# Order of an expert's half and quarter products, and row gathers shared by two experts, in a two-layer mixture-of-experts backbone

## The chip, the cores and the metric

The kernel runs on one core of a Trainium2 chip. The metric is the device time of one execution in microseconds. The engines are called as in the profile: PE is TensorE's matmul, PEld its weight load, DVE is VectorE, ACT is ScalarE, POOL is GpSimd, SP is SyncE, which issues most of the loads. SPq and POOLq are the queues of SP and POOL.

## What is computed

Two trunk layers over 512 latent tokens and 256 context tokens of width 1024. A layer mixes its tokens (a short convolution, a chunk gating, a neighbourhood attention, a latent attention), and then sends each token to two of 32 experts. The first layer routes 768 tokens, the second 512. What matters here is the expert stage:

```
gates = p_grp * jax.nn.softmax(top_v, axis=-1)
expert_id = (g_sel * EXPERTS_PER_GROUP + top_i).reshape(-1)
...
def expert_block(args):
    xb, e = args
    return (jax.nn.silu(xb @ w_gate[e]) * (xb @ w_up[e])) @ w_down[e]
...
y = y_buf[dest].reshape(n_tok, TOP_K_INNER, d).astype(jnp.float32) * gates[..., None]
return jnp.sum(y, axis=1).astype(h.dtype)
```

`w_gate` and `w_up` are 1024 x 512 for an expert, `w_down` 512 x 1024, all float32: 6 MB an expert, 201 MB a layer.

## The kernel before

`build` runs trunk and expert stage of the first layer, then of the second. The expert stage is `moe`. The routing ranks the experts by how many tokens they have; a table `CAP` of the program gives each rank a number of rows (first layer 2152 in all, second 1640), and tokens beyond it go through a loop for overflow blocks, whose number the device finds at run time (`nov`; all engines wait for it). `R["tok"]` is a table of 128 x 32 numbers: column r holds the token of each row of rank r, and a number out of bounds where there is none.

`seq` is the order of the products: gate and up of expert e, then down of expert e - 1. `load` walks along the same order ahead of PE and issues the weights from SP (line 147 in `unit2`) into slots, as far as slots are free: tiles `u` of 512 KB, and `xa`, `xb`, `xc`, of 1 MB, that hold two units. A unit holds two k of gate or up, or one k of down; a slot is free when the last product that reads it is done. SP issues in order, so a load whose slot is not free holds up all later ones. Loads of all queues share 16 DMA engines.

For each expert, `gather` lets POOL fetch its rows from `h2d` into one of three buffers `xb` (line 1704, by the indices in `R["tok"]`). `rows` turns them (PE transposes at line 1381 into `xTw`, a DVE copy at 1383 into `XT`). `gate_up` does both products, ACT the SiLU and DVE the product of the two (lines 1430 and 1431), `hT` turns the result, `down` does the third product, `rows_out` takes it out of PSUM, and POOL scatters the rows to `yd`. The rows of the last four ranks, 32 each, don't go through `yd`, but through a table of their own (`tail_scale`, `tail_rows`), and before them a scaling row `modd` is loaded behind the last scatter.

An expert's rows are the stationary operand of its products, the weights are streamed. `parts` cuts the rows by their number:

```
n = -(-W // QW)
return {1: [(0, QW)], 2: [(0, W)], 3: [(0, HW), (HW, QW)], 4: [(0, HW), (HW, HW)]}[n]
```

with HW = 64 and QW = 32. A part of more than 32 rows takes half of the array's columns, and its output columns are cut in two that run side by side ("halves", 512 columns each); a part of 32 rows or fewer takes a quarter, and its output is cut in four ("quarters", 256 columns). `streams` gives these pieces their places. Experts of 65 to 96 rows have one part of each kind: nine of the first layer, ten of the second. In `products` the loop over k is the outer one, so such an expert does, for each k, its halves and then its quarters:

```
for k in range(K):
    for a, w, o, b, m, c in S:
```

K is 8 for gate and up, 4 for down. The order in which each engine's instructions come is settled by a scheduler when the program is built; it may move an expert's products past each other. A product of float32 shows as two records of PE.

Of the kernel before, what the change touches and what calls it, by code (L numbers as in the profile page):

```python
# [11 lines left out]
I32 = mybir.dt.int32  # L12
# [9 lines left out]
NE = 32  # L22
# [41 lines left out]
HW = 64  # L64
# [30 lines left out]
class K:  # L95
# [886 lines left out]
    def project(self, l, ap, ah, yT, yM, TQ, w, wo, yc):  # L982
# [21 lines left out]
        br = ap.tile([128, M, 36], F32, name=f"brr{l}")  # L1004
        rows = ap.tile([32, 128], F32, name=f"mrow2{l}")
        nc.gpsimd.dma_start(rows, self.modd[l][1:3].rearrange("s m (k p) -> (s m k) p", p=128))
        lg = self.lg = self.small([128, TQ, 36], f"lg{l}", bufs=1)
        a2 = [self.bc(a2[m], l, 2, m) for m in range(M)]
# [58 lines left out]
        for t in range(TQ):  # L1067
# [8 lines left out]
            if t == 1:  # L1076
                ps = self.pss("br")
                with tc.issue_after(self.lastm.ins):
                    nc.tensor.transpose(ps[:, 0:32], rows, self.ident[0:32, 0:32])
                mc = ap.tile([128, 2, 2, 8], F32, name=f"mcol2{l}")  # L1080
                nc.vector.tensor_copy(mc.rearrange("p s m k -> p (s m k)"), ps[:, 0:32])
# [290 lines left out]
    def xt_tile(self, mp):  # L1372
        return mp.tile([128, D], F32, tag="XT", name=self.nm("XT"), bufs=2)

    def rows(self, mp, X, W):

        nc = self.nc
        ps = self.psw("xTw")
        Xv = X[0:W, :].rearrange("p (d k) -> p d k", k=8)
        for k in range(8):  # L1380
            nc.tensor.transpose(ps[:, k * 128:k * 128 + W], Xv[:, :, k], self.ident[0:W, 0:W])  # L1381
        xt = self.xt_tile(mp)[:, 0:8 * W].rearrange("p (k t) -> p k t", k=8)
        nc.vector.tensor_copy(xt, ps.rearrange("p (k n) -> p k n", k=8)[:, :, 0:W])  # L1383
        return xt
# [19 lines left out]
    def products(self, x, parts, ws, n, K, name):  # L1404


        S, out = [], []
        for a, w in parts:
            ps = self.pss(name)
            st = self.streams(ps, n, w, ws)  # L1410
            S += [(a, w) + y for y in st]
            out.append((ps, [y[0] for y in st]))
        for k in range(K):
            for a, w, o, b, m, c in S:
                q = m[0].shape[1]
                self.lastm = self.nc.tensor.matmul(o, x[:, k, a:a + w], m[k // q][:, k % q, c], start=(k == 0),  # L1416
                                                   stop=(k == K - 1), tile_position=(0, b))
        return out

    def gate_up(self, mp, xt, parts, wg, wu):  # L1420
# [81 lines left out]
    def overflow(self, l, R, src, pp, mp, XB):  # L1502
# [16 lines left out]
        with tc.For_i(0, n) as i:  # L1519
# [41 lines left out]
            nc.scalar.copy(xv, pv)  # L1561
            pg, pu = self.pss("over"), self.pss("over")
            products("g", [pg], xv)
            nc.scalar.activation(hh, pg[0:W, :], AF.Silu)
            products("u", [pu], xv)
            nc.vector.tensor_mul(hh, hh, pu[0:W, :])
            pt = self.pss("over")
# [28 lines left out]
    def moe(self, l):  # L1596
        nc, A, tc = self.nc, self.A, self.tc
        T = 6 if l == 0 else 4
        NB = 2 * T
        NA = 128 * NB  # L1600
# [3 lines left out]
        pp = ctx.enter_context(tc.tile_pool(name=f"mpp{l}", reuse_waits="tile", bufs=1, side=ms))  # L1604
# [12 lines left out]
        XB = [pp.tile([128, D], F32, name=f"xb{l}_{i}") for i in range(3)]  # L1617
# [4 lines left out]
        order = [0, 1]  # L1622
# [5 lines left out]
        while any(todo):  # L1628
            i = next(i for i in (range(len(COST))[::-1] if ahead > 0 else range(len(COST))) if todo[i])
# [3 lines left out]
        cap = [CAP[l][r] for r in order]  # L1633
        parts = [self.parts(w) for w in cap]
# [11 lines left out]
        for at, ts in ((("gu", NE - 2), range(0, T // 2)), (("d", NE - 3), range(T // 2, T))):  # L1646
            i = lseq.index(at) + 1
# [33 lines left out]
        def done_with(i):  # L1681
            for x in held.pop(seq[i]):
                x[1] = False

        xt, h, ht, X, written = {}, {}, {}, {}, []
        load(2)
        with tc.tile_pool(name=f"rt{l}", reuse_waits="tile", bufs=1, side=ms) as ap, tc.high_priority():
            R, rest = self.route(l, ap, pp)
# [8 lines left out]
        mp = ectx.enter_context(tc.tile_pool(name=f"moe{l}", reuse_waits="tile", bufs=1, side=ms))  # L1697
        self.rx = self.small([128, 6], "rx", bufs=1)

        def gather(e):  # L1700

            if e < NE:
                X[e] = XB[e % 3]
                self.lastp = nc.gpsimd.indirect_dma_start(  # L1704
                    out=X[e][0:cap[e], :], out_offset=None, in_=self.h2d[l][:, :],
                    in_offset=bass.IndirectOffsetOnAxis(ap=R["tok"][0:cap[e], order[e]:order[e] + 1], axis=0),
                    bounds_check=NA // 2 - 1, oob_is_err=False)

        def rows(e):
            if e < NE:  # L1710
                xt[e] = self.rows(mp, X.pop(e), parts[e][-1][0] + parts[e][-1][1])
                gather(e + 3)

        gather(0)
        self.overflow(l, R, src, pp, mp, XB[1:])
        gather(1)
        gather(2)
        fg = None
        if l == 1:

            g2 = [self.bc(self.bc_tile(pp), l, 3, 0)]
            fg = self.bc_tile(pp)
            nc.gpsimd.dma_start(fg, A["final_norm_g"].to_broadcast([128, D]))
        rows(0)
        load()
        tt = self.tail_table(l, pp, mp, R, T)
        acc = iter(range(T))
        na = dict(zip((("gu", NE - 2), ("d", NE - 3), ("gu", NE - 1), ("d", NE - 2)), (1, T // 3, T // 3, 1)))
        for i, (m, e) in enumerate(seq):
# [6 lines left out]
            else:  # L1736
# [5 lines left out]
                if j < 0:  # L1742
                    y = self.rows_out(mp, py, parts[e], g2[0] if l else None, cap[e])
                    nc.gpsimd.indirect_dma_start(  # L1744
                        out=self.yd[l][:, :], in_=y, in_offset=None,
                        out_offset=bass.IndirectOffsetOnAxis(ap=R["dst"][0:cap[e], order[e]:order[e] + 1], axis=0),
                        bounds_check=NA - 1, oob_is_err=False)
# [21 lines left out]
        for t in range(T):  # L1769
            ps = self.psw("tailw")  # L1770
# [168 lines left out]
```

## Time and profile before

| | us |
|---|---|
| runs: median (lowest to highest, 3 runs) | 1941.24 (1935.98 to 1943.87) |
| the profiled execution | 1937.65 |
| its span | 1935.9 |
| PE busy (12876 instructions) | 1778.4 |
| DVE, ACT, POOL busy | 740.0, 466.8, 234.3 |
| mean rate of the DMA engines over the span | 290 GB/s |

The first layer's expert stage lies from about 486 to 1065 us of the span, the second's from about 1400 to 1920. All rows below are of the profiled execution. A busy share is an average over stages that have different limits; what bounds a stage is read from the stage.

### The profile page before, as it was taken

What the parts mean: (1) busy time and instruction counts of PE and PEld (TensorE: products, weight loads), DVE (VectorE), ACT (ScalarE), POOL (GpSimd) and SP (SyncE); (2) the same over time, 40 slices, a digit from 0 to 9 for tenths busy, and PEclk for the clock granted to TensorE, in tenths of its full rate; (3) what the DMA queues carried; (4) which work ended last, traced back from release to release, by engine and by line L of the source; (5) the groups of instructions that cost most, each with busy time, mean ns of one, the idle gap of its engine ahead of it and who ended that gap; (6) DMA issues with size and microseconds to landing.
All of it is one profiled execution on the core that took longest, in us unless ns stands there. A gap on an engine that the chain in (4) does not pass through costs nothing. (4 is left out here: it accounts for less than half of the span.)

```text
span 1935.9 us, 32616 instructions
## 1 busy us (share of the span) xinstructions
PE 1778.4 (92%) x12876; PEld 973.3 (50%) x12876; DVE 740.0 (38%) x1599; ACT 466.8 (24%) x842; POOL 234.3 (12%) x267
## 2 busy tenths in 40 slices
PE   6999999996999999999986999999699999988994
PEld 3788788875334433333222688776434333333331
DVE  3666466555111110211105666665523232222225
ACT  4443464222111111111102555642200000000001
POOL 1000100132111111101001001002311011111010
PEclk9999999997999999999976999999799999999997
DMA  8368965534999999999849432528399999999995
GB/s 309 94 197 287 325 217 170 207 142 184 355 384 392 397 387 375 392 388 402 324 170 371 142 88 72 156 77 306 113 362 387 400 400 398 397 382 405 403 414 242
DMA packets 167101, 561.89 MB, mean 290 GB/s; under 512 B 20642, under 2 KB 47330, under 8 KB 137888
## 3 DMA queue, kind: packets, MB, share of 16 engines
q1 hardware_dynamic: 141616, 499.68, 68.7%
q0 software_dynamic: 21152, 54.16, 8.0%
q10 hardware_dynamic: 4176, 5.91, 0.9%
q8 instruction: 104, 1.70, 0.4%
q14 instruction: 53, 0.43, 0.1%
HBM read 533.54 MB, written 35.52 MB: 294 GB/s over the span
## 5 line engine op out<-in xcount | busy, mean ns | idle before, releaser
L1416 PE MATMUL gate_up<-u,XT 128*32 128x256 f32 (+4 forms) x1664 | 287.6, 493 | 5.9 <-DMA u<-in_w_up 4.1
L1416 PE MATMUL gate_up<-xb,XT 128*32 128x256 f32 (+4 forms) x1152 | 224.4, 489 | 10.4 <-DMA xb<-in_w_up 9.1
L1430 ACT ACTIVATE eh<-gate_up 64x256 f32<-64x256 f32 (+4 forms) x87 | 43.6, 501 | 788.0 <-PE gate_up L1416 774.4
L1383 DVE COPY XT<-xTw 128x256 f32<-128x256 f32 (+6 forms) x64 | 43.9, 689 | 449.2 <-PE gate_up L1416 433.0
L1416 PE MATMUL gate_up<-xa,XT 128*32 128x256 f32 (+4 forms) x680 | 156.9, 490 | 8.6 <-DMA xa<-in_w_up 8.4
L1416 PEld LDWEIGHTS gate_up<-u,XT 128*32 128x32 f32 (+4 forms) x1664 | 82.6, 121 | 160.7 <-issue 134.6
L194 PE MATMUL zunits<-hT,hi 128*128 128x512 f32 (+1 forms) x384 | 139.8, 365 | 0.9 <-ACT cqs L688 0.8
L195 PE MATMUL zunits<-hT,hi 128*128 128x512 f32 (+1 forms) x384 | 136.0, 354 | 0.0
L196 PE MATMUL zunits<-hT,lo 128*128 128x512 f32 (+1 forms) x384 | 135.3, 352 | 0.0
L1416 PE MATMUL gate_up<-xc,XT 128*32 128x256 f32 (+4 forms) x440 | 127.3, 498 | 2.8 <-DMA xc<-in_w_up 2.1
L1704 POOL DMA_INDIRECT xb<-h2d,tok x64 | 62.1, 971 | 528.1 <-PE xTw L1381 486.8
L1416 PEld LDWEIGHTS gate_up<-xb,XT 128*32 128x32 f32 (+4 forms) x1152 | 61.9, 121 | 123.6 <-issue 100.9
L1416 PE MATMUL down<-u,ehT 128*32 128x256 f32 (+4 forms) x656 | 111.6, 514 | 7.0 <-DMA u<-in_w_down 6.1
L1744 POOL DMA_INDIRECT yd<-ey,dst x56 | 52.9, 945 | 401.8 <-ACT ey L1473 215.6
L1431 DVE TENSOR_TENSOR eh<-eh,gate_up 64x256 f32<-64x256 f32 (+4 forms) x87 | 50.5, 580 | 131.3 <-ACT eh L1430 128.1
L1416 PE MATMUL down<-xb,ehT 128*32 128x256 f32 (+4 forms) x592 | 96.4, 498 | 2.6 <-DMA xb<-in_w_down 2.4
L1475 DVE TENSOR_TENSOR ey<-down,bc 32x256 f32<-32x256 f32 (+7 forms) x112 | 57.8, 516 | 102.1 <-PE down L1416 100.9
L1381 PE MATMUL xTw<-cpack,xb 96*128 96x96 f32 (+6 forms) x512 | 72.9, 282 | 20.4 <-DVE XT L1383 8.7
L1381 PEld LDWEIGHTS xTw<-cpack,xb 96*128 96x128 f32 (+6 forms) x512 | 63.1, 201 | 55.0 <-issue 24.0
L1473 ACT COPY ey<-down 64x512 f32<-64x512 f32 (+6 forms) x102 | 50.5, 495 | 157.2 <-PE down L1416 156.1
L175 DVE TENSOR_TENSOR lo<-u,hi 128x1024 fp32r<-128x1024 f32 (+2 forms) x54 | 65.6, 1217 | 46.6 <-ACT hi L169 44.1
L1416 PEld LDWEIGHTS gate_up<-xa,XT 128*32 128x32 f32 (+4 forms) x680 | 40.2, 119 | 85.8 <-issue 70.9
(395 smaller groups left out, 2876.5 us busy)
## 6 DMA issues: line engine op xcount, KB each, us to landing
u<-in_w_gate SPq DMA_DIRECT2D x112, 512.0 KB
u<-in_w_up SPq DMA_DIRECT2D x106, 512.0 KB
u<-in_w_ada SPq DMA_DIRECT2D x96, 512.0 KB
u<-in_w_down SPq DMA_DIRECT2D x89, 512.0 KB
xb<-in_w_gate SPq DMA_DIRECT2D x37, 1024.0 KB
xb<-in_w_down SPq DMA_DIRECT2D x37, 1024.0 KB
xb<-in_w_up SPq DMA_DIRECT2D x35, 1024.0 KB
xa<-in_w_down SPq DMA_DIRECT2D x26, 1024.0 KB
```

The costliest lines, as they stand in the source:

```text
L175: self.nc.vector.tensor_sub(o, v, h.bitcast(F32))
L194: mm(out, a[0], b[0], start=start, stop=False)
L195: mm(out, a[0], b[1], start=False, stop=False)
L196: self.lastm = mm(out, a[1], b[0], start=False, stop=stop)
L1381: nc.tensor.transpose(ps[:, k * 128:k * 128 + W], Xv[:, :, k], self.ident[0:W, 0:W])
L1383: nc.vector.tensor_copy(xt, ps.rearrange("p (k n) -> p k n", k=8)[:, :, 0:W])
L1416: self.lastm = self.nc.tensor.matmul(o, x[:, k, a:a + w], m[k // q][:, k % q, c], start=(k == 0), stop=(k == K - 1), tile_position=(0, b))
L1431: self.lastv = nc.vector.tensor_mul(v, v, ps[64:64 + r, 0:c])
L1473: self.nc.scalar.copy(y[a:a + w, c], p[0:w, :])
L1475: self.nc.vector.tensor_mul(y[a:a + w, c], p[0:w, :], g2[b:b + w, c])
L1704: self.lastp = nc.gpsimd.indirect_dma_start(out=X[e][0:cap[e], :], out_offset=None, in_=self.h2d[l][:, :], in_offset=bass.IndirectOffsetOn ...
L1744: nc.gpsimd.indirect_dma_start(out=self.yd[l][:, :], in_=y, in_offset=None, out_offset=bass.IndirectOffsetOnAxis(ap=R["dst"][0:cap[e], ord ...
```

## The change

Two parts. `products` now takes the parts of an expert one after the other, with the loop over k inside: all halves of the 64 rows, then all quarters of the other 32. And rows are gathered by groups: two experts that follow each other and have at most 64 rows each form a group, any other expert is one by itself. A gather always names 128 rows. For a group of two the indices of both, 64 each, are copied by DVE into a column of a table `gi`, and the second expert's rows land on partitions 64 to 127, from where `rows` turns them. There are 26 groups in the first layer and 24 in the second, for 32 and 32 gathers before.

```diff
-    def rows(self, mp, X, W):
+    def rows(self, mp, X, a, W):
...
-        Xv = X[0:W, :].rearrange("p (d k) -> p d k", k=8)
+        Xv = X[a:a + W, :].rearrange("p (d k) -> p d k", k=8)
         for k in range(8):
-            nc.tensor.transpose(ps[:, k * 128:k * 128 + W], Xv[:, :, k], self.ident[0:W, 0:W])
+            nc.tensor.transpose(ps[:, k * 128:k * 128 + W], Xv[:, :, k], self.ident[a:a + W, a:a + W])
...
-        S, out = [], []
+        out = []
         for a, w in parts:
             ps = self.pss(name)
             st = self.streams(ps, n, w, ws)
-            S += [(a, w) + y for y in st]
+            for k in range(K):
+                for o, b, m, c in st:
+                    q = m[0].shape[1]
+                    self.lastm = self.nc.tensor.matmul(o, x[:, k, a:a + w], m[k // q][:, k % q, c], start=(k == 0),
+                                                       stop=(k == K - 1), tile_position=(0, b))
             out.append((ps, [y[0] for y in st]))
-        for k in range(K):
-            for a, w, o, b, m, c in S:
-                q = m[0].shape[1]
-                self.lastm = self.nc.tensor.matmul(o, x[:, k, a:a + w], m[k // q][:, k % q, c], start=(k == 0),
-                                                   stop=(k == K - 1), tile_position=(0, b))
         return out
...
+        groups, place, e = [], {}, 0
+        while e < NE:
+            n = 2 if e + 1 < NE and max(cap[e], cap[e + 1]) <= HW else 1
+            for i in range(n):
+                place[e + i] = len(groups), HW * i
+            groups.append(range(e, e + n))
+            e += n
...
-        def gather(e):
-
-            if e < NE:
-                X[e] = XB[e % 3]
-                self.lastp = nc.gpsimd.indirect_dma_start(
-                    out=X[e][0:cap[e], :], out_offset=None, in_=self.h2d[l][:, :],
-                    in_offset=bass.IndirectOffsetOnAxis(ap=R["tok"][0:cap[e], order[e]:order[e] + 1], axis=0),
-                    bounds_check=NA // 2 - 1, oob_is_err=False)
+        gi = pp.tile([128, len(groups)], I32, name=f"gi{l}")
+
+        def gather(g):
+
+            if g >= len(groups):
+                return
+            X[g] = XB[g % 3]
+            if len(groups[g]) == 1:
+                r = order[groups[g][0]]
+                ix = R["tok"][:, r:r + 1]
+            else:
+                ix = gi[:, g:g + 1]
+                for i, e in enumerate(groups[g]):
+                    nc.vector.tensor_copy(ix[HW * i:HW * i + HW], R["tok"][0:HW, order[e]:order[e] + 1])
+            nc.gpsimd.indirect_dma_start(out=X[g], out_offset=None, in_=self.h2d[l][:, :],
+                                         in_offset=bass.IndirectOffsetOnAxis(ap=ix, axis=0),
+                                         bounds_check=NA // 2 - 1, oob_is_err=False)
...
-                xt[e] = self.rows(mp, X.pop(e), parts[e][-1][0] + parts[e][-1][1])
-                gather(e + 3)
+                g, a = place[e]
+                xt[e] = self.rows(mp, X[g], a, parts[e][-1][0] + parts[e][-1][1])
+                if e == groups[g][-1]:
+                    gather(g + 3)
```

How the instructions move, at three places. On PE, the gate and up product of the first layer's second expert (96 rows), in the kernel before; the weights are in tiles `xa` and `xb`, 64x512 is a half and 32x256 a quarter, and x2 stands for two alike:

```order
L1416 MATMUL gate_up_5621<-xa_1_5078,XT_5598 64x512
L1416 MATMUL gate_up_5621<-xa_2_5079,XT_5598 64x512
L1416 MATMUL gate_up_5622<-xa_1_5078,XT_5598 32x256 x2
L1416 MATMUL gate_up_5622<-xa_2_5079,XT_5598 32x256 x2
L1416 MATMUL gate_up_5621<-xb_0_5082,XT_5598 64x512
L1416 MATMUL gate_up_5621<-xb_1_5083,XT_5598 64x512
L1416 MATMUL gate_up_5622<-xb_0_5082,XT_5598 32x256 x2
L1416 MATMUL gate_up_5622<-xb_1_5083,XT_5598 32x256 x2
```

and in the changed kernel:

```order
L1414 MATMUL gate_up_5624<-xa_1_5078,XT_5599 64x512
L1414 MATMUL gate_up_5624<-xa_2_5079,XT_5599 64x512
L1414 MATMUL gate_up_5624<-xb_0_5082,XT_5599 64x512
L1414 MATMUL gate_up_5624<-xb_1_5083,XT_5599 64x512
...
L1414 MATMUL gate_up_5641<-xa_1_5078,XT_5599 32x256 x2
L1414 MATMUL gate_up_5641<-xa_2_5079,XT_5599 32x256 x2
...
L1414 MATMUL gate_up_5641<-xb_0_5082,XT_5599 32x256 x2
L1414 MATMUL gate_up_5641<-xb_1_5083,XT_5599 32x256 x2
```

Before, halves and quarters take turns for each k; now sixteen halves come first, and the quarters follow.

On POOL, the first layer's gathers after the overflow loop (the DMA into `xb` from `h2d`), before:

```order
L1704 DMA xb_1_5102<-h2d_110,tok_5238 96x1024
L1704 DMA xb_2_5103<-h2d_110,tok_5238 32x1024
L1704 DMA xb_0_5101<-h2d_110,tok_5238 128x1024
L1704 DMA xb_1_5102<-h2d_110,tok_5238 64x1024
L1704 DMA xb_2_5103<-h2d_110,tok_5238 64x1024
```

and now, where `gi` in place of `tok` marks a gather for two experts:

```order
L1721 DMA xb_1_5102<-h2d_110,tok_5238 128x1024
L1721 DMA xb_2_5103<-h2d_110,tok_5238 128x1024
L1721 DMA xb_0_5101<-h2d_110,tok_5238 128x1024
L1721 DMA xb_1_5102<-h2d_110,gi_5274 128x1024
L1721 DMA xb_2_5103<-h2d_110,tok_5238 128x1024
```

The gathers name 128 rows each; the one for the two experts of 64 rows has taken the place of two.

On DVE, the end of the first layer's routing, where `nb` and `nov` lead to the number of overflow blocks, in the changed kernel; the copies into `gi` are new, and `tlim` stood ahead of `nb` before:

```order
L1330 CAST tpos_7336<-posi_5254 128x12
L1270 TENSOR_SCALAR more_5256<-cpack,col_5249 32x6
L1720 COPY gi_5274<-tok_5238 64x1 x2
L1271 TENSOR_REDUCE nb_5257<-more_5256 32x1
L1720 COPY gi_5274<-tok_5238 64x1 x4
L1275 CAST nov_5262<-route_5260 1x1
L1720 COPY gi_5274<-tok_5238 64x1 x2
L1321 TENSOR_TENSOR tlim_7121<-col_5249,cpack 32x1
L1720 COPY gi_5274<-tok_5238 64x1 x4
```

Two copies have come ahead of `nb`, four between it and `nov`, and six behind.

## Rows read from the trace of the kernel before

**Rows 1.** The page: PE's busy time; the rate in 40 equal slices.

```profile
PE 1778.4 (92%) x12876; PEld 973.3 (50%) x12876; DVE 740.0 (38%) x1599; ACT 466.8 (24%) x842; POOL 234.3 (12%) x267
...
GB/s 309 94 197 287 325 217 170 207 142 184 355 384 392 397 387 375 392 388 402 324 170 371 142 88 72 156 77 306 113 362 387 400 400 398 397 382 405 403 414 242
```

**Rows 2.** Stretches: us, busy us by engine, granted clock, DMA share, GB/s.

```profile
486.00:940.00 454.00, 446.86 (x2520) 160.41 (x2520) 66.67 (x130) 64.41 (x127) 52.47 (x55) 0.99 1.01 386
940.00:1065.00 125.00, 99.83 (x783) 32.13 (x782) 35.97 (x58) 20.55 (x35) 9.28 (x15) 0.79 0.73 275
1402.00:1705.00 303.00, 289.23 (x2350) 106.11 (x2352) 84.35 (x190) 12.51 (x27) 39.70 (x42) 0.98 1.01 390
1705.00:1912.00 207.00, 178.88 (x1148) 62.60 (x1143) 52.12 (x97) 11.19 (x22) 18.47 (x22) 0.93 1.00 401
```

**Rows 3.** Waits of PE, 500 to 990 us: total, times, longest.

```profile
PE hT L1450 <- DVE ehT L1452: 3.1, 6, 0.5
...
PE down L1416 <- DVE ehT L1452: 0.2, 1, 0.2
```

**Rows 4.** Waits of PE, 990 to 1065 us.

```profile
PE tail_scalew L1366 <- DMA u<-modd: 5.9, 1, 5.9
```

**Rows 5.** Waits of PE, 1402 to 1700 and 1700 to 1912 us: first line of each.

```profile
PE hT L1450 <- DVE ehT L1452: 6.8, 5, 1.8
...
PE gate_up L1416 <- DMA xa<-in_w_up: 8.4, 2, 7.1
```

**Rows 6.** The chain that ended last, from 1700 us: start, us, what.

```profile
1705.74 18.26 DMA xb<-in_w_down
...
1883.50 21.39 DMA xa<-in_w_up
```

**Rows 7.** Timeline of PE in a mixed expert, first layer: start, us, instruction.

```profile
840.88 0.41 PE L1416 MATMUL gate_up<-xa,XT 128*32 128x256 f32 x2
...
841.12 0.39 PE L1416 MATMUL gate_up<-xa,XT 128*32 128x256 f32 x2
...
841.45 0.64 PE L1416 MATMUL gate_up<-xa,XT 128*64 128x512 f32 x1
...
841.93 0.59 PE L1416 MATMUL gate_up<-xa,XT 128*64 128x512 f32 x1
...
842.46 0.41 PE L1416 MATMUL gate_up<-xa,XT 128*32 128x256 f32 x2
```

**Rows 8.** Timeline: halves alone; the chain: mixed product, product of quarters alone.

```profile
573.53 0.59 PE L1416 MATMUL gate_up<-xb,XT 128*64 128x512 f32 x1
...
573.96 0.59 PE L1416 MATMUL gate_up<-xb,XT 128*64 128x512 f32 x1
...
1419.07 12.70 PE gate_up L1416 x96
...
1440.97 3.45 PE gate_up L1416 x64
```

**Rows 9.** Timeline of SP's issues at the end of the first layer.

```profile
985.43 1.91 SPq L147 DMA_DIRECT2D u<-in_w_up  x2
1014.30 0.33 SPq L147 DMA_DIRECT2D xa<-in_w_down  x1
```

**Rows 10.** The page's group of gathers: busy, mean ns, idle before.

```profile
L1704 POOL DMA_INDIRECT xb<-h2d,tok x64 | 62.1, 971 | 528.1 <-PE xTw L1381 486.8
```

**Rows 11.** DMA, 479 to 484 us: packets, MB, share, of the first gather.

```profile
q0 software_dynamic: 112, 0.14, 11.8%
```

**Rows 12.** Timeline of DVE at the end of the first routing.

```profile
478.06 0.14 DVE L1321 TENSOR_TENSOR tlim<-col,cpack 32x1 f32<-32x1 f32 x1
478.18 0.15 DVE L1271 TENSOR_REDUCE nb<-more 32x1 f32<-32x6 f32 x1
478.69 0.15 DVE L1275 CAST nov<-route 1x1 int32<-1x1 f32 x1 [0.37 <-PE route L1273]
```

**Rows 13.** Waits of SP, 1440 to 1705 us: total, times, longest.

```profile
SPq L147 <- PE down L1416: 13.5, 8, 6.8
```

## The prediction

> **What bounds the kernel now.** I read four views in this order: the page's lines of busy time and of rate by slice, the busy times by stretch, the waits of TensorE (PE) in each stretch, and the chain that ended last. The page shows PE busy for 92% of the span, and rates near 400 GB/s in the slices of the two expert stages [rows 1]. An average over stages cannot say which of the two sets the time, so the stretches come next [rows 2]. In the first layer's expert stage, from 486 to 940 us, both are full: PE busy 446.86 of 454 us, DMA share 1.01. From 940 to 1065 the DMA share is 0.73, so there the loads follow PE. In the second layer's, 1402 to 1912 us, the share is 1.01 and then 1.00 to the end.
>
> The waits separate them. Between 500 and 990 us PE's waits fill six lines, 6.9 us in all, and no DMA is among them; the first and the last of the six stand in [rows 3]. So the first layer is bound by PE: whatever its products lose or gain there moves everything behind. At 996.7 PE waits for a broadcast that GpSimd (POOL) issues behind the last scatter [rows 4]; that DMA is itself late by what PE is late, and shifts with it. In the second layer PE waits for no DMA from 1402 to 1700, but after that it does, up to 7.1 us at once [rows 5], and the chain of work that ended last leaves PE at 1705.74 for a load of 18.26 us, and near the end runs over a load from 1883.50 on, 21.39 us [rows 6]. PE there runs into a DMA queue that has been full since 1402. So the second layer ends when its loads have landed.
>
> **What a change of tile shape costs.** An expert of 65 to 96 rows has a part of 64 rows (two products side by side, "halves", 512 columns) and one of 32 rows (four, "quarters", 256 columns). The kernel now does for each k the halves and then the quarters. [Rows 7] show one k-step: quarters at 840.88 and 841.12, halves at 841.45 and 841.93, quarters again at 842.46, each product in two passes. One whole step is 842.46 - 840.88 = 1.58 us. Where halves follow halves, a pass takes 573.96 - 573.53 = 0.43 us; sixteen passes of quarters alone take 3.45 us, 0.216 each [rows 8]. Without a change of shape the step would be 2 x 0.43 + 2 x 0.216 = 1.29 us. The two changes in it cost 0.29 us.
>
> **The change part by part.** *Order of products.* In the order of instructions, as it is put out for both kernels, the first layer has 121 steps from halves to quarters and 100 back before, and 47 and 26 now: 74 pairs fewer. In the second it is 132 and 114 before, 50 and 32 now: 82 fewer. (Nine and ten such experts, twelve k-steps each; the scheduler still splits a product in two where it expects its weights late, and mixes it with other products, so that not all go.) First layer: 74 x 0.29 = 21.5 us off PE, all of it where PE waits for no load: **-21.5 us**. The bounds are 0, if the loss does not go with the order, and 9 experts x 10 pairs x 0.29 = 26 us, if only one change per product were left. A few halves stand alone in both orders, without a partner on the other half of the array; I count them as equal. Second layer: 82 x 0.29 = 23.8 us off PE, beside DMA that is full: **0**. The cover is the queue of loads; where it to run faster, part of this would count (a rival below).
>
> *What is late next in the first layer.* The closest PE comes to its loads is before 940, where DMA is saturated. Two of the nine experts stand at the start (5.8 us of the 21.5), the other seven from the eighteenth expert on. After that the loads had been waiting for PE: share 0.73 in the last stretch, that is 0.27 x 125 = 34 us of idle DMA, and SyncE (SP) stands from 987.34 to 1014.30 with a load whose place PE has not freed [rows 9]. I take it that the gain passes through.
>
> *Weights are held longer.* With all halves first, the unit of weights for the first k is read until the quarters come by. In the first layer SP is then nearer to its places being free than now, since PE is earlier; 0 in the sum, priced as a rival.
>
> *Gathers.* There are 14 fewer (50 for 64). POOL takes 0.97 us for one and waits 486.8 us for PE before them [rows 10], so nothing is on the path: 0. Each now names 128 rows. A row past an expert's tokens has an index out of bounds and moves nothing of size: the first gather, of 96 rows, left 112 packets with 0.14 MB [rows 11], about 33 rows of 4 KB. So the 2608 further rows (26 x 128 - 2152 and 24 x 128 - 1640) bring next to no bytes. Bounds: nothing, or as full rows 1432 x 4 KB at 390 GB/s = 15 us in the layer where DMA is the end; I take 0, as the packets show. If the cover went, a gather that is late would hold the transposes of two experts; it is issued three groups ahead, which is more experts than now.
>
> *Transposes from the upper half.* The second expert of a pair is turned from partitions 64 on. Their number stays. No row shows this transpose there; I take 0, with bounds of a tenth of a microsecond to either side for each of the 14 pairs.
>
> *Copies of indices.* VectorE (DVE) gets 28 copies of 64 numbers. Two stand ahead of the sum of blocks and four ahead of the number of overflow blocks, on which all engines wait before the expert stage. Instructions of that size follow each other by 0.12 us, and the second place has 0.37 us of idle time in which four nearly fit [rows 12]. So 0.3 us a layer: **+0.6 us** (bounds 0 and 1.4).
>
> **Sum.** The profiled execution took 1937.65 us: 1937.65 - 21.5 + 0.6 = 1916.8. That execution lies 3.6 us under the median of the runs, and the four times shown spread over 7.9 us; I add half of the 3.6 and forecast **1919 us**.
>
> **Rivals.** *A: the second layer gains too.* For: from 1402 to 1705 DMA moves 390 GB/s, and the best slice of the page, in the same layer, 414 [rows 1, 2]. If what holds the rate down is PE's pace, the same bytes at 414 take 303 x (1 - 390/414) = 17.5 us less: 1901 us. Against: the share of 1.01 says that every engine has a packet at every moment, and SP waits there mostly for earlier loads; its largest line on PE is 13.5 us in 8 waits for the down product [rows 13]. Chance 0.12. The Trainium skill ("HBM Reference", Specifications) puts a core that streams alone at about 425 GB/s; by that figure a layer at 390 would have room for all that PE gives back, and the time would be about 1895, an estimate; no slice of this profile reaches that rate.
>
> *B: a load becomes the wait in the first layer.* PE overtakes its loads before 940, where DMA has nothing to spare. Then only the idle DMA of the last stretch counts, 34 us less the 27 of SP's long wait, which stays: a gain of 7 us, 1933 us. For: both resources are full in that stretch. Against: no wait for a load in 490 us, so there is a stock of unknown size. Chance 0.16.
>
> *C, slower: weights held to the end of a product starve the loads of the second layer.* A unit of gate or up weights (two k) is free after 2 x 1.58 = 3.2 us now, and after 8 x 0.86 + 0.15 + 2 x 0.43 = 7.9 with the change, 4.7 later; one of the down product (one k) after 4.0 in place of 1.6, 2.4 later. Ten experts: 71 us of later issue, in the layer that ends with its loads. It decides if more than 21 of these 71 us become idle DMA, that is, a share under 0.96 there; at half, 35 us: 1954 us. Against: SP has several loads under way and rarely waits for PE there [rows 13]. Chance 0.05.
>
> **How the numbers follow.** Forecast 0.67, A 0.12, B 0.16, C 0.05. A measurement of this kernel can tell about 0.5% from no change, 9.7 us, so the forecast and A are faster (0.79), B is no change (0.16), C is slower (0.05). The range reaches from A to B, 1900 to 1934, and leaves out C, the far end of A and a weaker B; the forecast's own range is 1911 to 1927, from its bounds and the spread of the runs.
>
> **What would show it.** In the profile after: a mixed expert's gate and up product takes about 10.5 us and not 12.70 [rows 8]; the expert stage of the first layer, 486 to 1065 us before, is some 21 us shorter, and PE still waits for no load in it until the broadcast; the second layer's stage, 1402 to 1912 us before, stays near 510 us with a share of 1.0, and PE's waits for loads there, few before 1700 now, grow by about 20 us and begin earlier. I am wrong if PE waits for loads in the first layer (B), if the second layer's rate rises above 400 GB/s (A), if its DMA share falls (C), or if the step from halves to quarters costs as much once per product as now in twelve.

## The result, and the profile after

The changed kernel takes **1895.09 us** (median of 4 runs, 1892.86 to 1898.18), the one before 1942.18 (4 runs): ratio **0.9764**, 95% interval 0.9738 to 0.9790. I forecast 1919 and a range of 1900 to 1934. The direction was right; the gain is twice the forecast and lies 5 us outside the range. The profiled execution took 1894.95 us, its span is 1893.2.

From the start of the first product of an expert stage to the start of the last, the first layer goes from 577.1 us (486.9 to 1064.0) to 543.2 (489.0 to 1032.2), the second from 514.1 (1402.5 to 1916.6) to 503.3 (1369.9 to 1873.2). That is -33.9 and -10.8; all that lies around the stages adds 2 us. I had -21.5 and 0.

The page after, lines of PE's busy time and of the rate by slice, answers to [rows 1]:

```profile
PE 1730.5 (91%) x12876; PEld 999.2 (53%) x12876; DVE 744.1 (39%) x1627; ACT 467.2 (25%) x842; POOL 221.7 (12%) x253
...
GB/s 305 107 188 275 318 227 184 160 211 141 339 414 407 399 398 396 398 401 411 387 229 319 147 87 106 140 76 303 129 366 411 414 410 411 404 401 404 409 414 226
```

Busy times of the stretches of both stages in the changed kernel, columns as in [rows 2]:

```profile
489.00:910.00 421.00, 418.20 (x2466) 163.64 (x2470) 63.06 (x124) 62.34 (x123) 45.89 (x48) 0.99 1.01 404
910.00:1033.00 123.00, 97.34 (x844) 38.09 (x835) 38.38 (x63) 22.73 (x40) 9.71 (x15) 0.83 0.86 323
1370.00:1660.00 290.00, 272.12 (x2352) 117.83 (x2352) 83.98 (x189) 12.53 (x27) 34.75 (x36) 0.98 1.00 403
1660.00:1873.00 213.00, 178.02 (x1172) 66.34 (x1174) 54.97 (x102) 11.21 (x22) 15.62 (x19) 0.90 0.98 395
```

PE is busy 48 us less. The line that I did not foresee is the last column: the first stretch moves 404 GB/s where it moved 386, at the same share of 1.01. The bytes are the same, 561.89 MB before and 561.90 after.

PE's timeline of the second expert of the first layer (65 to 96 rows), after: halves of gate and up, then their quarters.

```profile
503.90 3.65 PE L1414 MATMUL gate_up<-xa,XT 128*64 128x512 f32 x16
507.38 3.60 PE L1414 MATMUL gate_up<-xb,XT 128*64 128x512 f32 x16
510.92 1.93 PE L1414 MATMUL gate_up<-xa,XT 128*32 128x256 f32 x32
512.67 1.91 PE L1414 MATMUL gate_up<-xb,XT 128*32 128x256 f32 x32
```

The product lasts from 503.90 to 514.58, 10.68 us, where one of its size took 12.70 in the kernel before [rows 8]: 2.02 us, seven pairs of changes of shape at 0.29. I had said about 10.5.

PE's waits from 500 to 960 us, after, all of them; they answer to [rows 3]:

```profile
PE hT L1449 <- DVE ehT L1451: 2.6, 5, 0.5
PE xTw L1381 <- DVE XT L1383: 0.7, 1, 0.7
```

So the first layer still waits for no load, although PE is faster. In the second layer the chain leaves PE for the loads much earlier than in [rows 6], where that was at 1705.74. The chain after, rows from its stretch from 1369 us on:

```profile
1405.01 3.45 PE gate_up L1414 x64
...
1418.74 6.65 DMA xc<-in_w_up
...
1439.10 17.14 DMA u<-in_w_gate
1456.36 18.33 DMA xc<-in_w_gate
```

From 1418.74 on this chain is mostly loads. PE's waits for loads in this stage grow from 18.7 to 30.5 us in all, by 12 us and not by the 20 that I had. The second layer is bound by its loads, as I said, but its loads run faster.

**Where the rate comes from.** The view of DMA over one gather shows it. First the kernel before, 737.5 to 740.5 us, in which a gather of 80 rows lands beside the loads (packets, MB, share of the 16 engines' time):

```profile
DMA packets 236, 0.87 MB, mean 290 GB/s; under 512 B 56, under 2 KB 56, under 8 KB 204
...
q1 hardware_dynamic: 126, 0.57, 66.6%
q0 software_dynamic: 110, 0.30, 36.0%
```

Then the change, 727.3 to 730.3 us, where a gather of 128 rows for an expert of a similar size lands (some packets of a scatter are in both windows):

```profile
DMA packets 346, 1.21 MB, mean 403 GB/s; under 512 B 106, under 2 KB 106, under 8 KB 291
...
q1 hardware_dynamic: 177, 0.86, 70.3%
q0 software_dynamic: 168, 0.34, 29.5%
```

Three microseconds of 16 engines are 48. Before, the gather had 36.0% of them for 0.30 MB, or 73 rows of 4 KB: 0.24 us a row; the loads had 66.6% for 139 times 4 KB: 0.23 us each. After, it is 0.17 and 0.16 us. The engines have a packet at every moment in both, but before each packet takes 1.4 times as long, **the loads' packets as well**. Over the three microseconds the rate is 290 and not 403.

To count this over the stages I gave the packets of the gathers' queue, in order of time, to the gathers and scatters by their numbers of rows (a scatter of 40 rows that stands alone leaves 80 packets, one of 72 leaves 112, and so a number of rows that is no multiple of 16 is filled up), and took the mean time of a gather's 4 KB packets. Before it is 208 ns in both layers (172 for the first layer's gathers that name 128 rows there), after 166 and 167; the loads' packets that start while a gather's rows land took 207 and 202 ns per 4 KB before, and 162 after. The assignment is rough where a gather and a scatter overlap. The scatters name 32 to 128 rows in the first layer of both kernels and their packets take 161 to 163 ns; loads beside a scatter alone take 159 to 163 ns. In the change a scatter of 80 rows lands from 898.2 to 906 us while the DMA engines move 418 GB/s:

```profile
q0 software_dynamic: 96, 0.28, 9.1%
```

So it is the gathers, which write into the on-chip tiles, and not every transfer of fewer than 128 rows. A plainer count needs no such assignment: in the kernel before, the 4-us slices from 490 to 940 us move 377 GB/s where they hold packets of the gathers' queue and 402 where they don't; in the change, from 490 to 910, 404 and 401.

### The profile page after: what moved, and what is told of

Read it like the earlier page. It is cut to its first block, busy times and chain, and to the rows that moved or that the text cites. A ratio compares the mean times of both kernels' runs of the same rounds, so it can differ in the third digit from the quotient of the medians.

```text
span 1893.2 us, 32583 instructions
## 1 busy us (share of the span) xinstructions
PE 1730.5 (91%) x12876; PEld 999.2 (53%) x12876; DVE 744.1 (39%) x1627; ACT 467.2 (25%) x842; POOL 221.7 (12%) x253
## 2 busy tenths in 40 slices
DMA packets 169022, 561.90 MB, mean 297 GB/s; under 512 B 22562, under 2 KB 49250, under 8 KB 139808
## 4 chain that ended last, share of the span: by engine, by line
PE 25%; DMA 18%; DVE 3%; issue 3%; ACT 1%; POOL 0%; SPq 0%; POOLq 0%; ACTq 0%; DVEq 0%
DMA u<-in_w_down 6%; PE gate_up L1414 6%; PE down L1414 3%; DMA u<-in_w_gate 3%; PE zunits L194 2%; PE zunits L195 2%; PE zunits L196 2%; DMA u<-in_w_up 2%; DMA xb<-in_w_down 2%; DMA xb<-in_w_up 1%; DMA xa<-in_w_up 1%; PE transP L838 1%; DMA xc<-in_w_gate 1%; DMA xc<-in_w_up 1%; PE tailw L1791 1%
## 5 line engine op out<-in xcount | busy, mean ns | idle before, releaser
L1414 PE MATMUL gate_up<-u,XT 128*32 128x256 f32 (+4 forms) x1664 | 277.3, 489 | 12.3 <-DMA u<-in_w_up 9.2
L1414 PE MATMUL gate_up<-xb,XT 128*32 128x256 f32 (+4 forms) x1152 | 215.0, 483 | 12.0 <-DMA xb<-in_w_up 10.6
L1414 PEld LDWEIGHTS gate_up<-u,XT 128*32 128x32 f32 (+4 forms) x1664 | 92.2, 123 | 149.3 <-issue 106.9
L1414 PE MATMUL gate_up<-xa,XT 128*32 128x256 f32 (+4 forms) x680 | 149.8, 488 | 5.3 <-DMA xa<-in_w_up 2.9
L1414 PEld LDWEIGHTS gate_up<-xb,XT 128*32 128x32 f32 (+4 forms) x1152 | 69.1, 121 | 112.1 <-issue 80.1
L1414 PE MATMUL down<-xb,ehT 128*32 128x256 f32 (+4 forms) x592 | 91.9, 490 | 5.6 <-DMA xb<-in_w_down 5.6
L1381 PEld LDWEIGHTS xTw<-cpack,xb 96*128 96x128 f32 (+6 forms) x512 | 61.7, 200 | 51.8 <-issue 22.8
L1381 PE MATMUL xTw<-cpack,xb 96*128 96x96 f32 (+6 forms) x512 | 72.1, 283 | 17.7 <-DVE XT L1383 7.0
L175 DVE TENSOR_TENSOR lo<-u,hi 128x1024 fp32r<-128x1024 f32 (+2 forms) x54 | 65.5, 1217 | 46.0 <-ACT hi L169 45.4
L194 PEld LDWEIGHTS zunits<-hT,hi 128*128 128x128 f32 x384 | 72.8, 190 | 16.0 <-issue 4.4
L1451 DVE COPY ehT<-hT 128x256 f32<-128x256 f32 (+4 forms) x47 | 19.6, 418 | 154.2 <-PE hT L1449 153.7
```

Source lines behind the costliest of these rows:

```text
L175: self.nc.vector.tensor_sub(o, v, h.bitcast(F32))
L194: mm(out, a[0], b[0], start=start, stop=False)
```

## The experiments

**Theory.** Two gains. The order of products takes some 24 us of PE off the first layer. Gathers of fewer than 128 rows slow the packets in flight, and 128 rows end that. **Rivals:** the rate rises since PE comes earlier (my rival A); or what counts is that there are 14 gathers fewer.

The first four runs part these. All stage times below go from the start of the first expert product to the start of the last.

**1. The order alone.**

```diff
 kernel before, products():
-        for k in range(K):
-            for a, w, o, b, m, c in S:
+            for k in range(K):
+                for o, b, m, c in st:
```

> The new order of products with the gathers of before. Theory (two separate gains: the order takes some 24 us of PE off the first layer's stage; gathers of fewer than 128 rows slow all packets in flight, and 128 rows end that): the rate stays as before, near 386 and 390 GB/s in the two expert stages, a 4 KB packet of a gather takes about 190 ns; first layer's products 15 to 30 us shorter, second layer's stage still 510 to 516 us; 1912 to 1925 us. Rival A (the rate follows PE's pace): rate 402 in both stages, second stage near 503 us, 1893 to 1900 us.

Measured: 1921.18 us, ratio 0.9905 (0.9887 to 0.9922); stages 559.0 and 512.6 us. Rival A falls: 380 us of the second stage (the busy times from 1444 us on, columns as in [rows 2]) run at 399 GB/s,

```profile
1444.00:1824.00 380.00, 342.75 (x2383) 132.60 (x2383) 93.96 (x202) 15.66 (x33) 41.94 (x44) 0.98 1.01 399
```

and the same stretch of the kernel before at 398:

```profile
1460.00:1840.00 380.00, 356.25 (x2460) 126.20 (x2458) 96.95 (x210) 16.03 (x34) 43.98 (x46) 0.98 1.01 398
```

The gathers' packets still take 206 and 205 ns. And PE now meets its loads in the first layer; its waits for DMA from 500 to 975 us:

```profile
PE gate_up L1414 <- DMA xc<-in_w_up: 2.4, 1, 2.4
PE down L1414 <- DMA xb<-in_w_down: 1.4, 3, 0.5
PE gate_up L1414 <- DMA xb<-in_w_gate: 1.3, 2, 0.7
PE gate_up L1414 <- DMA xb<-in_w_up: 0.9, 2, 0.6
```

That is 6.0 us, where neither the kernel before nor the change has any. The stage is 18.1 us shorter, with these waits in it: this is the mechanism of my rival B, a load that becomes the wait, in a small size.

**2. The gathers alone.**

```diff
 changed kernel, products(): as in the kernel before
-            for k in range(K):
-                for o, b, m, c in st:
+        for k in range(K):
+            for a, w, o, b, m, c in S:
```

> The new gathers with the order of products of before. Theory: rate of the second layer's stage 400 to 405 GB/s and the stage 8 to 14 us shorter than before; first layer's stage within 6 us of before, since PE sets it; packets of a gather about 162 ns; 1925 to 1934 us. Rival A: rate 386 to 391 as before, 1938 to 1944 us.

Measured: 1930.40 us, ratio 0.9946 (0.9927 to 0.9964); stages 574.8 and 508.2 us; the gathers' packets 165 and 171 ns. Busy times of 380 us in the second stage:

```profile
1460.00:1840.00 380.00, 359.93 (x2518) 127.59 (x2506) 99.32 (x215) 16.41 (x35) 38.33 (x40) 0.98 1.01 408
```

So the gathers alone lift the rate from 398 to 408. The second stage gains 5.9 us, less than I wrote down. The first, where PE sets the time, gains 2.3.

Alone the parts give 19.3 and 10.0 us, together 45. The rest is that they need each other, in the first layer above all: 18.1 and 2.3 us apart, 33.9 together, 13.5 more than the sum. The order makes PE catch up with its loads, and the faster loads let it run: that is the 6.0 us of waits. The rest of these 13.5 us lies in the transposes between the products (60.0 us up to the broadcast in the order alone, 53.8 in the change) and behind the broadcast (65.5 and 61.7 us); why these two need both parts is not shown.

**3. Is it the rows or the number of gathers?** One gather for each expert, each of 128 rows.

```diff
-            n = 2 if e + 1 < NE and max(cap[e], cap[e + 1]) <= HW else 1
+            n = 1
```

> The change, but one gather for each expert, each of 128 rows: 64 gathers in place of 50, no copies of indices, no transposes from the upper half. Theory (the number of rows in a gather decides): packets of a gather about 162 ns, rates 400 to 405, 1890 to 1900 us. Rival (the 14 fewer gathers or the pairing decide): packets about 190 ns, rates 386 to 391, 1912 to 1925 us.

Measured: 1904.24 us, ratio 0.9819 (0.9800 to 0.9837); the packets take 165 and 167 ns. With 64 gathers, as many as before, 17 of the 26 us that separate the order alone from the change are there. The rows decide the packet's time. The time lies between the two expectations: pairing is worth another 7 to 9 us.

**4. Other numbers of rows.**

```diff
 rows128_single:
+                W = (96, 112, 120)[g % 3] if l else 64 if cap[g] <= 64 else 128
-                ix = R["tok"][:, r:r + 1]
+                ix = R["tok"][0:W, r:r + 1]
-            nc.gpsimd.indirect_dma_start(out=X[g], ...
+            nc.gpsimd.indirect_dma_start(out=X[g][0:W, :], ...
```

> As rows128_single, but gathers in the first layer of 64 rows where an expert has up to 64 and 128 otherwise, and in the second of 96, 112 and 120 rows in turn. Theory: first layer, 64 rows 180 to 200 ns a packet, 128 rows about 162; second layer, all three sizes over 180 ns and its rate near 391 GB/s; 1900 to 1915 us. If only small gathers are slow: 96 to 120 rows about 162 ns and the second stage near 503 us.

Measured: 1928.40 us, ratio 0.9942 (0.9920 to 0.9964); stages 552.5 and 528.1. In the first layer a packet of a 64-row gather takes 220 ns and one of a 128-row gather 167; in the second 96, 112 and 120 rows take 202, 195 and 200. So it is not small gathers that are slow: 120 rows are slow as well, and 128 are not. The time, 1928.40, misses what I expected (1900 to 1915). The stage with 96 to 120 rows is even 14 us longer than before the change, where the gathers named no more rows than the expert has places. Busy times of 380 us in it:

```profile
1437.00:1817.00 380.00, 335.05 (x2289) 127.73 (x2290) 91.08 (x196) 15.30 (x32) 42.40 (x44) 0.96 0.99 383
```

Here the share is under 1 too: packets are slow, and engines are without one at times.

**5. Pairs by two gathers of 64 rows**, one into each half of the tile.

```diff
-            nc.gpsimd.indirect_dma_start(out=X[g], ...
+            for a, W, y in ([(0, 128, ix)] if len(groups[g]) == 1 else
+                            [(HW * i, HW, R["tok"][:, order[e]:order[e] + 1]) for i, e in enumerate(groups[g])]):
+                nc.gpsimd.indirect_dma_start(out=X[g][a:a + W, :], ...
```

> The change, but each pair is fetched by two gathers of 64 rows, one into the lower and one into the upper half of the same tile: 64 gathers, transposes from the upper half as in the change. Theory (any split of a gather other than 128 rows slows all packets in flight): packets of the 64-row gathers 180 to 200 ns, those of the 128-row ones about 162; 1908 to 1922 us. Rival (only the lower half is slow, or only the count of gathers matters): packets 160 to 165 ns, about 1904 us as rows128_single.

Measured: 1905.66 us, ratio 0.9826 (0.9812 to 0.9839). Within this one kernel packets of the 64-row gathers take 226 and 208 ns in the two layers, those of the 128-row ones 166 and 170. The packets are the theory's, but the time is near the rival's, so only the packets part the two. Against the change (0.9764, 0.9738 to 0.9790) the split of 14 pairs costs some 10 us, clear of the noise.

**6. and 7. What a skipped row costs.** Behind each gather of the change a second one whose indices are all out of bounds, of 128 and of 16 rows.

```diff
+            nc.gpsimd.indirect_dma_start(out=dump[0:128, :], out_offset=None,
+                                         in_=self.h2d[l].rearrange("a (b c) -> (a b) c", c=16),
+                                         in_offset=bass.IndirectOffsetOnAxis(ap=far[0:128, :], axis=0),
+                                         bounds_check=NA // 2 - 1, oob_is_err=False)
```

> The change, with a second gather behind each of its 50, of 128 rows whose indices are all out of bounds, so that it moves no row. It asks what a skipped row costs. Theory (the 9 us between 64 single gathers and 50 paired ones are the price of 14 gathers and their skipped rows, some 0.6 us each): 1910 to 1928 us. Rival (a skipped row costs nothing, as the 4-byte packets of about 9 ns suggest): 1894 to 1900 us.

> As skip128, with 16 rows in each of the 50 added gathers. If the rows make the price: 1895 to 1901 us, an eighth of what skip128 adds. If the gather itself (issue, its completion) makes it: the same as skip128.

Measured: 1965.49 and 1961.97 us (ratios 1.0150 and 1.0113). The first misses on both of its readings, and the second comes out as "the same as skip128" for a reason that it did not name, a fault of the experiment: all added gathers have one target, so that each waits for the one before, and the real gathers behind them come late. With 16 rows, POOL's waits from 488 to 990 us and PE's from 1400 to 1700 show it:

```profile
POOL dump L1727 <- DMA dump<-h2d,far: 81.4, 20, 7.9
...
PE xTw L1381 <- DMA xb<-h2d,tok: 16.7, 2, 10.3
```

Only the difference can be read: 50 x 112 = 5600 more skipped rows cost 3.5 us by the medians (7 by the ratios). The change skips 2608 more rows than the kernel before; by these runs that is some 2 to 3 us. That they bring next to nothing was right.

**8. What pairing is worth.** An even load of the engines? Every second expert of up to 64 rows in the upper half.

```diff
 rows128_single:
-                place[e + i] = len(groups), HW * i
+                place[e + i] = len(groups), HW * (e % 2 if cap[e] <= HW else 0)
...
+                nc.vector.memset(ix[0:HW], 1 << 20)
+                nc.vector.tensor_copy(ix[HW:128], R["tok"][0:HW, r:r + 1])
```

> As rows128_single (one gather of 128 rows for each expert), but every second expert of up to 64 rows lies in the upper half of its tile, its index list padded below. It asks why 14 fewer gathers are worth 9 us. Theory (a gather whose rows all lie in the lower half loads only some of the DMA engines, and the others go idle; two experts on both halves even this out): idle DMA time in the stages smaller than in rows128_single, 1896 to 1902 us. If the count of gathers decides: 1903 to 1906 us.

Measured: 1897.73 us, ratio 0.9789 (0.9765 to 0.9813), where the change on the same chip took 1896.82 (0.9775, 0.9752 to 0.9799). With 64 gathers, so their count is not it. This fits the theory, but the next run does not.

**9. All of them in the upper half.**

```diff
 single_alt:
-                place[e + i] = len(groups), HW * (e % 2 if cap[e] <= HW else 0)
+                place[e + i] = len(groups), HW * (cap[e] <= HW)
```

> As single_alt, but every expert of up to 64 rows lies in the upper half. Theory (two gathers in a row that load the same half of the DMA engines leave the others idle; taking turns evens this out): the rate of the second stage as in rows128_single, about 403 GB/s, and 1902 to 1907 us. Rival (the lower half is the slow one, whatever the order): the rate as in single_alt, 407 GB/s or more, and 1893 to 1899 us.

Measured: 1892.71 us, ratio 0.9769 (0.9746 to 0.9792); the change on this chip 1895.02 (0.9773). My theory of taking turns falls. 180 us of the second stage, in which all experts but the first have 33 to 64 places, tell the three placings apart, in busy times: all in the lower half (rows128_single),

```profile
1590.00:1770.00 180.00, 163.20 (x840) 58.60 (x836) 41.72 (x90) 7.40 (x15) 21.66 (x22) 0.97 1.00 399
```

by turns (single_alt),

```profile
1585.00:1765.00 180.00, 165.73 (x848) 59.14 (x846) 45.08 (x95) 8.00 (x16) 22.33 (x23) 0.97 1.01 407
```

all in the upper half (single_up):

```profile
1586.00:1766.00 180.00, 165.08 (x856) 59.19 (x854) 43.35 (x92) 7.98 (x16) 21.62 (x22) 0.96 1.02 411
```

The more rows in the upper half, the higher the rate. These are one profile each; three profiles of the change, which has rows in both halves, show 404 to 406 GB/s in the same 180 us. It is not the gathers' packet time: that is 166 or 167 ns in the second layer of all three. Of 90 slices of 2 us in such a stretch, 10, 6 and 0 have a share under 0.97. What else keeps the lower half's part of DMA busy is not shown; the scatters, which start at partition 0 in all these kernels, would fit. No run moved them.

**10. Is the order worth nothing in the second layer?**

```diff
+        if self.layer == 1:
+            return self.products_by_turns(x, parts, ws, n, K, name)
```

> The change, but in the second layer the order of products of before. It asks what the new order is worth there once the gathers are fast. If the second layer is bound by its loads alone, as I forecast, the order is worth nothing there: 1893 to 1898 us, second stage 503 us. From the stage of gathers_only (508 us) against the change's (503): 1898 to 1902 us. If PE's pace sets the rate (rival A): 1905 us or more.

Measured: 1898.32 us, ratio 0.9793 (0.9775 to 0.9811), on the border of the first two readings: 1.5 us over the change on the same chip, within the noise; second stage 505.3 us against 501.8 there. The rate is that of the change although PE is busy 9 us more in the 380; this run, then the change:

```profile
1431.00:1811.00 380.00, 359.68 (x2482) 127.42 (x2482) 97.57 (x212) 16.08 (x34) 37.45 (x39) 0.97 1.01 409
...
1427.00:1807.00 380.00, 350.28 (x2527) 137.57 (x2520) 99.52 (x214) 17.02 (x36) 36.37 (x38) 0.98 1.01 408
```

**11. Fuller gathers.** An expert of up to 32 rows also behind one of up to 96, three of 32 together: 41 gathers.

```diff
-            n = 2 if e + 1 < NE and max(cap[e], cap[e + 1]) <= HW else 1
+            n = at = 0
+            while e + n < NE:
+                w = parts[e + n][-1][0] + parts[e + n][-1][1]
+                a = -(-at // QW) * QW
+                if QW < w <= HW:
+                    a = -(-at // HW) * HW
+                if a + w > 128 or at and w > HW:
+                    break
+                place[e + n] = len(groups), a
+                at, n = a + w, n + 1
```

> The change, with the 128 rows filled further: an expert of up to 32 rows also behind one of up to 96, and three of 32 rows in one gather: 41 gathers in place of 50, 24 to 17 of them in the second layer. If a gather costs 0.3 to 0.6 us of DMA that is full: 1889 to 1893 us. If a gather and its skipped rows cost nothing: 1894 to 1897 us. Slower than 1897 if the added copies of indices before the expert stage cost more than that.

> The same kernel as join, on the chip of the next run: 1886 to 1892 us, 3 to 8 under the change beside it, if its packing is worth something; equal to it within 2 us if the difference before was between chips.

> The change itself, beside join_again on one chip: 1892 to 1898 us, some 3 to 8 us above it if packing more experts into a gather is worth something.

Measured: 1888.95 us, ratio 0.9742 (0.9729 to 0.9756); on a second chip 1890.81 (0.9746, 0.9729 to 0.9763), beside 1895.02 for the change there (0.9773, 0.9752 to 0.9794). It lies 6 us under the change's first result and 4 under its result on the same chip; the intervals still overlap. It is the fastest version found; clear of noise against the kernel before, not against the change. Its 380 us of the second stage run at 410 GB/s:

```profile
1428.00:1808.00 380.00, 351.56 (x2530) 138.60 (x2526) 100.66 (x216) 17.02 (x36) 33.13 (x35) 0.98 1.01 410
```

**12. Fewer changes of shape still.** As join, but the down product does its quarters first.

```diff
-        for a, w in parts:
+        for a, w in parts if name != "down" else parts[::-1]:
```

> As join, and the down product does its quarters first and its halves behind them, so that a mixed expert goes halves, quarters, quarters, halves. It saves up to one change of shape per product. If the first layer is still bound by PE: some 18 changes of 0.15 us, 1 to 4 us under join, 1885 to 1889 us. If weights held longer or the loads end it: 1888 to 1893 us.

Measured: 1909.16 us, ratio 0.9843 (0.9825 to 0.9861), 20 us worse than join: both readings miss. In the first layer's order there are 40 steps from halves to quarters and 38 back, in join 47 and 26: nothing was saved, since transposes stand between. Its first stage is 556.3 us and join's 542.8; which of the new neighbours costs that I did not follow up. The change itself ran once more beside run 8:

> The change itself, beside the others on one chip: 1893 to 1898 us. If join was faster by its packing and not by its chip, this stays 4 to 9 us above join's 1889.

## Why the prediction was right and wrong

*What bounds the kernel.* Right: the first layer by PE, the second by its loads. Wrong was what I made of the share of 1.01. I wrote that **every engine has a packet at every moment** and took this for a full queue that can't run faster. The share counts the time in which a packet is under way. A packet that takes 230 ns for what others do in 160 fills the share just as well. The sign was in [rows 1] and [rows 2]: a mean of 386 and 390 GB/s beside slices of 414, all at a share of 1. The best slice, from 1839 to 1887 us, lies behind the last gather, which POOL issues at 1795.7.

*Order of products, -21.5.* Right. Up to the broadcast of [rows 4] the first layer's products became 22.2 us shorter (gate and up 16.2, down 6.0), measured from one pass's start to the next. The stage lost 33.9. Of the rest 6.1 us lie in the transposes between the products; why is not shown. The other 5.6 lie behind the broadcast, where PE waits as long as before (17.7 and 17.8 us) and the granted clock, a mean over both of its levels, is 0.69 in place of 0.65. That the gain passes through holds for the change, but not for the order alone, which has 6.0 us in waits for loads; that the term came out in full is in part the doing of the gathers, which I had put at 0.

*Second layer, 0 for the order.* Right within the noise: run 10.

*Weights held longer, and rival C.* Right that it costs nothing: the share stays at 1.00 in the first 290 us of the second stage.

***Gathers, 0.* This step failed.** I asked what the 14 gathers fewer save POOL, and what the rows skipped add in bytes. Both answers were near enough (run 8: 64 gathers took as long as 50; runs 6 and 7: 2 to 3 us for the rows). I did not ask what the gathers of before cost the other packets. My bounds for them ran from nothing to 15 us slower; no row that I had excluded a gain, and the rate of the slices with and without gathers, 377 and 402, was there to be read. The term measured -10.0 us alone (run 2), and some -26 beside the new order (1921.18 to 1895.09). In the first layer it is what let the order pass through, in the second it is most of the gain: without the new order there the stage still takes 505.3 us (run 10), where it took 514.1.

The Trainium skill has a rule that bears on this ("DMA: Bandwidth & Descriptors", The descriptor swizzle): a transfer of 128 partitions is split so that each DMA engine writes one port of the on-chip memory. Another page of the Trainium skill ("SBUF — State Buffer", Door 1: The DMA port swizzle) maps the partitions to 16 ports. If another number of rows is split in another way, two engines can meet at a port, and a load is held up with the gather. The traces agree in what such a rule would give (164 to 171 ns at 128 rows; 195 to 226 at 64, 96, 112 and 120). They carry no engine's number, so that the ports are the cause is not shown. By the same map rows in partitions 0 to 63 reach only 8 of the ports, and rows in 64 to 127 the other 8. So the map does not tell the halves apart, where run 9 does (399 against 411 GB/s), and what does is not shown.

*Transposes from the upper half, 0.* Nothing in the runs speaks against it. *Copies of indices, +0.6.* Right. DVE's timeline at the end of the first routing, after, answers to [rows 12]:

```profile
480.73 0.29 DVE L1720 COPY gi<-tok 64x1 int32<-64x1 int32 x2
...
481.13 0.61 DVE L1720 COPY gi<-tok 64x1 int32<-64x1 int32 x4
481.77 0.15 DVE L1275 CAST nov<-route 1x1 int32<-1x1 f32 x1
```

From the index list (480.44) to the number of blocks it is now 1.33 us; before it was 0.92 (477.77 to 478.69): 0.4 us a layer.

*Rivals.* A had the time (1901) and a rate of 414 as its price, but the wrong mechanism: PE's pace leaves the rate alone (run 1). The sign that I had set for A, a rate above 400 GB/s in the second layer, did appear. I gave 0.12 to a higher rate because I tied it to that mechanism. B was there in the order alone, 6 us, and the faster loads took it away.

## What to carry to other kernels

A DMA share near 1 says that packets are under way, not that they are fast: divide the share by the bytes, queue by queue, in a window with a gather and in one without. In this kernel a gather should name 128 rows also where the expert has far fewer, since skipped rows are nearly free and the other numbers that were tried (64, 96, 112, 120) slow the loads beside it. And where two resources are both nearly full in a stretch, a gain on one may pay in full only with a gain on the other: here 18 and 2 us apart, 34 together.

## What the runs showed that I had not expected

- A gather of 64, 96, 112 or 120 rows stretches its own packets from about 166 ns to 195 to 226 in the mean, and the loads' packets beside it with them; one of 128 rows does not, even if three quarters of its rows are skipped. Scatters of 32 to 128 rows do not either.
- 5600 more skipped rows added 3.5 us by the medians, 7 by the ratios.
- Rows gathered into partitions 64 to 127 cost the loads less than rows in 0 to 63: 411, 407 and 399 GB/s with all, every second and no expert of up to 64 rows there, in one profile each.
- Gathers behind one another on one target tile hold up the whole expert stage: 50 of them cost some 67 us with hardly a byte moved.
